# Latent queries of an encoder layer: rotary rows of four heads in one tile, the latent row factor as the exponent's scale

## The chip, the core and the metric

The kernel runs on one core of a Trainium2 chip. A core has a matrix engine (PE, with its weight loads listed apart as PEld), a vector engine (DVE), a scalar engine (ACT), a general engine (POOL), a queue engine that issues DMAs (SP), and 16 DMA engines. The engines run side by side and wait for one another by semaphores. The metric is the device time of one execution in microseconds, and less is better.

## The reference

The reference is one layer of a streaming encoder for 1024 prompt rows and 32 sample rows (1056 columns in the kernel, which keeps activations transposed). The branch that matters here is multi-head latent attention with 8 heads. Queries come from a latent of 384 numbers, keys and values from a latent of 256; a query and a key have 64 plain columns ("nope") and 32 columns that are turned by a rotary table; the turned key is shared by all heads.

```python
q = (rms_norm(q_lat, g_q_lat) @ w_uq).reshape(B, T, H_A, NOPE + ROPE)   # 384 -> 8 heads x (64 + 32)
q_nope = q[..., :NOPE]
q_rope = apply_rope(q[..., NOPE:], cos, sin)     # (x1*cos - x2*sin, x2*cos + x1*sin), halves of 16
...
s = (einsum(q_nope, k_nope) + einsum(q_rope, k_rope)) * MLA_SCALE       # 96 ** -0.5
p = softmax(where(mask, s, NEG))                  # block-causal, blocks of 64 rows
out = einsum(p, v)
```

The norm of the query latent divides each row by one number, its root mean square. That division is the "latent row factor": it is the same for all columns and all heads of a row, so it can be applied to the latent, to the queries, or to the scores.

## The kernel before

The work is in float32 precision by pairs: a matrix is split into a high and a low part, and a product is three matmuls (lines 75 to 77: high by high, low by high, high by low). `hi` (line 68) is an ACT copy, `lo` (line 71) a DVE subtraction.

The latent attention runs over four pairs of heads (`p` = 0 to 3). Before a pair's attention, its *expansion* has made queries, keys and (once for two pairs) values. Expansion 0 runs before the loop, as a stage of its own; expansion p + 1 is spread as fill work through the attention of pair p. An order is written out as a list of short names, and PE, ACT and DVE follow it for the work inside attention; elsewhere a scheduler orders the instructions of each engine by dependencies and its own estimates. Names in the list: S scores of a block, M its maximum, m the minimum of two pieces' negated maxima, E the exponent, R and C the reciprocal and the scaling, T transposes, h and v their high and low copies, V the product with values, o and p the output's copies and store; and as fill x and z (query matmuls of the pair's first and second head), X (queries times the table), J and j (high and low part of the finished queries, QH and QL), y, H, L (keys: matmuls, high, low), Z, I, i (sample rows and weight splits). U, W, w, f and G are fill from the output projection of the other branch. The digits after a name are the block of 128 query rows, and, after the point, the head of the pair.

Queries before: each head has a tile of 128 rows, 64 nope, 32 rotary, and the same 32 with halves swapped (the weight columns are gathered that way by `PARTS`, line 42). That takes 9 matmuls for each of three column blocks of 352, so 27 per head and 54 per pair. Line 1405 multiplies the tile, straight out of PSUM, by a table `qt` whose rows hold 96^-0.5, the cosines, and the signed sines. The row factor `qr` (one value per column, spread to 128 partitions by a DMA) is multiplied into that table at line 1480. The keys' tile has its 32 rotary rows twice, so the contraction over 128 rows sums both halves of the rotation. The scores then are QH and QL against KH and KL (lines 1510 to 1515), and the exponent (line 915) takes a bias, the negated maximum, and no scale.

PSUM has eight banks: three named s, two mm, two tr, one pv. SBUF tiles named big (three) and A (five) are shared by many steps.

## Time and profile before

| | us |
|---|---|
| median of three runs | 1690.74 (1689.0 to 1691.93) |
| the profiled execution, whole | 1689.64 |
| its span in the profile | 1687.8 |
| expansion 0 (keys, values, queries of pair 0) | 569.5 to 587.2 |
| attention of pair 0, with expansion 1 | 587.2 to 645.4 |
| attention of pair 1, with expansion 2 | 645.4 to 705.5 |
| attention of pair 2, with expansion 3 | 705.5 to some 766 |

Times are counted from the start of the span. A row of the timeline gives start, duration, engine, line of the kernel, operation, and output<-inputs with shapes; the brackets behind it give the idle time ahead of it on that engine, with what ended it. Listed durations of matmuls overlap, since the array is pipelined, so the rate of a run of matmuls is read from their starts. Rows of DMAs give the size of one and the median time from issue to landing.

### The profile page before, as it was taken

The numbers are of one execution on the slowest core, as the hardware profiler recorded it, in microseconds if no ns is written. First come the engines' busy times: TensorE is split into PE (matmuls) and PEld (weight loads), VectorE is DVE, ScalarE is ACT, GpSimd is POOL, SyncE is SP. The second block draws the span as 40 slices with busy tenths as digits, with TensorE's granted clock in tenths as the row PEclk, the third lists the DMA queues.
The fourth block names the chain that finished last, engine by engine and source line by source line (L and its number), as shares of the span: only waits on it lengthen the run. The fifth ranks groups of instructions, "written<-read, shape, count | busy, mean of one in ns | idle before, by whom it ended". The sixth has DMA issues, their size and how long they took to land. (4 is left out here: it accounts for less than half of the span.)

```text
span 1687.8 us, 30267 instructions
## 1 busy us (share of the span) xinstructions
PE 1650.3 (98%) x11646; PEld 1514.1 (90%) x11646; DVE 1268.5 (75%) x2121; ACT 995.0 (59%) x1945; POOL 294.9 (17%) x569
## 2 busy tenths in 40 slices
PE   5999999999999999999999999999999999999997
PEld 3999999999998898998988799999999999877885
DVE  4865698989873777877766789877787777787456
ACT  4545687978874677776762575444444444545442
POOL 3113312111110311111000212212112112200013
PEclk8999999999999999999999999999999999999999
DMA  9335876576532521221374523433333333697643
GB/s 337 101 125 187 281 239 165 168 198 174 174 112 57 147 68 44 81 70 50 130 241 137 194 91 100 151 107 120 131 109 118 132 110 116 241 333 237 207 141 122
DMA packets 185729, 255.22 MB, mean 151 GB/s; under 512 B 14702, under 2 KB 125056, under 8 KB 185584
## 3 DMA queue, kind: packets, MB, share of 16 engines
q1 hardware_dynamic: 164944, 194.11, 36.8%
q0 software_dynamic: 20416, 59.08, 10.1%
q8 instruction: 92, 1.51, 0.4%
q14 instruction: 53, 0.43, 0.1%
q10 hardware_dynamic: 224, 0.09, 0.0%
HBM read 187.86 MB, written 64.57 MB: 150 GB/s over the span
## 5 line engine op out<-in xcount | busy, mean ns | idle before, releaser
L68 ACT ACTIVATE wh<-wr 128x1024 fp32r<-128x1024 f32 (+5 forms) x163 | 132.1, 819 | 226.2 <-PE s L2066 82.4
L71 DVE TENSOR_TENSOR wl<-wr,wh 128x1024 fp32r<-128x1024 f32 (+5 forms) x163 | 150.2, 929 | 80.6 <-ACT wh L68 80.5
L75 PE MATMUL mm<-hh,wh 128*128 128x352 f32 x456 | 152.3, 334 | 0.0
L76 PE MATMUL mm<-hl,wh 128*128 128x352 f32 x456 | 148.7, 326 | 0.4 <-DVE hl L333 0.3
L77 PE MATMUL mm<-hh,wl 128*128 128x352 f32 x456 | 148.3, 325 | 0.0
L2065 PE MATMUL mm<-T,wh 128*128 128x256 f32 (+1 forms) x376 | 108.1, 288 | 0.0
L2067 PE MATMUL mm<-T,wl 128*128 128x256 f32 (+1 forms) x376 | 107.1, 285 | 0.4 <-DVE wl L71 0.2
L2066 PE MATMUL mm<-T,wh 128*128 128x256 f32 (+1 forms) x376 | 106.6, 284 | 0.0
L2067 PE MATMUL s<-T,wl 128*128 128x256 f32 (+1 forms) x348 | 99.3, 285 | 0.0
L2065 PE MATMUL s<-T,wh 128*128 128x256 f32 (+1 forms) x348 | 99.2, 285 | 0.0
L2066 PE MATMUL s<-T,wh 128*128 128x256 f32 (+1 forms) x348 | 98.8, 284 | 0.0
L71 DVE TENSOR_TENSOR wl<-S,wh 128x1024 fp32r<-128x1024 f32 (+1 forms) x55 | 59.2, 1078 | 50.3 <-ACT wh L68 49.9
L76 PEld LDWEIGHTS mm<-hl,wh 128*128 128x128 f32 x456 | 86.4, 189 | 3.5 <-DVE hl L333 1.8
L75 PEld LDWEIGHTS mm<-hh,wh 128*128 128x128 f32 x456 | 86.3, 189 | 3.4 <-issue 2.1
L2206 DVE SCALAR_TENSOR_TENSOR u<-u,c,u 128x1058 f32<-128x1058 f32 x68 | 87.1, 1318 | 2.0 <-ACT u L2203 0.7
L77 PEld LDWEIGHTS mm<-hh,wl 128*128 128x128 f32 x456 | 86.3, 189 | 0.2
L806 PE MATMUL tr<-c,A 128*128 128x128 f32 x576 | 85.0, 272 | 0.3 <-DVE A L922 0.3
L68 ACT ACTIVATE wh<-S 128x1024 fp32r<-128x1024 f32 (+1 forms) x55 | 51.8, 944 | 48.4 <-PE s L2066 13.4
L2067 PE MATMUL tr<-T,wl 128*128 128x272 f32 (+1 forms) x272 | 77.7, 286 | 0.3 <-DVE wl L71 0.3
L2065 PE MATMUL tr<-T,wh 128*128 128x272 f32 (+1 forms) x272 | 77.8, 286 | 0.0
L2066 PE MATMUL tr<-T,wh 128*128 128x272 f32 (+1 forms) x272 | 77.3, 284 | 0.0
L2196 POOL COPY c<-u 128x2 f32<-128x2 f32 x44 | 26.6, 604 | 266.6 <-DVE u L2142 230.5
(760 smaller groups left out, 5831.5 us busy)
## 6 DMA issues: line engine op xcount, KB each, us to landing
wr<-in_w_up_dram SPq DMA_DIRECT2D x44, 512.0 KB, 4.2
dr<-in_w_down_dram SPq DMA_DIRECT2D x43, 512.0 KB, 5.4
wr<-in_w_in_dram SPq DMA_DIRECT2D x33, 512.0 KB, 6.7
A<-in_w_ada_dram SPq DMA_DIRECT2D x32, 512.0 KB, 6.2
wr<-gdn SPq DMA_DIRECT2D x30, 512.0 KB, 4.5
gdn<-u POOLq DMA_DIRECT2D x23, 512.0 KB, 5.2
gd<-nat POOLq DMA_DIRECT2D x48, 176.0 KB, 3.5
t<-gd SPq DMA_DIRECT2D x16, 528.0 KB, 6.0
```

The source lines that it names most:

```text
L68: self.nc.scalar.activation(out, in_, AF.Identity, scale=scale)
L71: return self.nc.vector.tensor_tensor(out, full, hi.bitcast(F32), ALU.subtract)
L75: m(ps, lh, rh, start=start, stop=False)
L76: m(ps, lh, rl, start=False, stop=False)
L77: self.pe = m(ps, ll, rh, start=False, stop=stop).ins
L806: self.nc.tensor.transpose(tr[:, (2 * s + q) * P : (2 * s + q + 1) * P], at[q][:, b * P : b * P + P], self.idt)
L2065: m(ps[:, :n], w[0][:, k], x[0][:, k, c], start=first and k == 0, stop=False, skip_group_check=True)
L2066: m(ps[:, :n], w[0][:, k], x[1][:, k, c], start=False, stop=False, skip_group_check=True)
L2067: i = m(ps[:, :n], w[1][:, k], x[0][:, k, c], start=False, stop=k == 3, skip_group_check=True)
L2196: nc.gpsimd.tensor_copy(self.CV[:, 0:2, cc], u[:, 1024:1026])
L2206: nc.vector.scalar_tensor_tensor(y, u[:, w : w + YW], self.cvT[:, w, cc : cc + 1], y, ALU.mult, ALU.add)
```

## The change

Queries: `queries()` now has the 64 nope columns of both heads in one 128-row tile, 27 matmuls per pair. `rotary()` has the 32 rotary columns of four heads in another, 27 matmuls, and is done in expansions 0 (heads 0 to 3) and 1 (heads 4 to 7) alone. `turned()` multiplies that tile by a cosine table and by a sine table (six DVE products of 128x352), and writes both results to DRAM (`rqc` and `rqs`, 528 KB each). `rows()` loads, for each head of a pair, its 32 rows of either into rows 64 to 128 of the head's query tile (four DMAs of 132 KB). The nope rows are copied from PSUM with the factor 96^-0.5, head 0 by DVE (X), head 1 by ACT (K).

Keys: the second copy of the rotary rows is now swapped in its halves of 16, so it meets the sine products of unswapped queries. This takes 15 copies on POOL's queue where 10 were, and 3 loads of the cached keys where 2 were.

Row factor: it is no longer multiplied into the table. It is loaded as columns (`qs`, one per block of 128 query rows, by five DMAs in place of one that spreads a row), and is the exponent's `scale`. The maximum must carry it as well: m becomes one operation with both, and a new DVE step n (128x1) stands behind M for the 32 blocks whose scores are in one piece.

Also: the table is loaded by 12 DMAs in place of one; the weights of an expansion by six (pairs 0 and 1) or three in place of two, and split by one operation each on ACT and DVE; the transposes of the cached latents (line 1607) stand ahead of pair 2 in place of pair 1. The order has a list of its own for pair 0 with the rotary matmuls (z) and products (B) of expansion 1 in its middle; the z of the tail are gone from all lists.

```diff
-PARTS = ((0, 0, 96), (96, 80, 16), (112, 64, 16))
+QS = 96 ** -0.5
...
+    ORDER_0 = """
...
+        f2 E4.1b f G f v3.0 z z z B B z z z B B z z z B B x s4.1 S5.1a M5.0b R4.1 m5.0 V3.0 C4.1
...
-        V5.0 T6.1 o5 T6.0 h6.1 R7.1 p5 y C7.1 h6.0 v6.1 z v6.0 H z H L V6.1 V6.0 L T7.0 o6 z h7.0 p6 z X z v7.0
-        z y X V7.0 y o7 p7 z H z H L z L X Z J j
+        y v5.0 J V5.2 M7.1 n7.1 V5.1 Z E7.1 j V5.0 T6.1 o5 T6.0 h6.1 R7.1 p5 y C7.1 h6.0 v6.1 v6.0 H H L V6.1
+        V6.0 L T7.0 o6 h7.0 p6 v7.0 y V7.0 y o7 p7 H H L L Z J j
...
             elif k == "m":
-                vec.tensor_tensor(mx[:, 0:1], mx[:, 0:1], mx[:, 1:2], ALU.min)
+                vec.scalar_tensor_tensor(mx[:, 0:1], mx[:, 0:1], mx[:, 1:2], self.qs[:, 2 * u + i : 2 * u + i + 1],
+                                         ALU.min, ALU.mult)
+            elif k == "n":
+                vec.tensor_tensor(mx[:, 0:1], mx[:, 0:1], self.qs[:, 2 * u + i : 2 * u + i + 1], ALU.mult)
             elif k == "E":
                 self.exp = nc.scalar.activation(A[:, c0 : c0 + m], banks[x][:, :m], AF.Exp, bias=mx[:, 0:1],
-                                                accum_out=sm[:, j : j + 1])
+                                                scale=self.qs[:, 2 * u + i : 2 * u + i + 1], accum_out=sm[:, j : j + 1])
...
-            def queries(e):
+            def queries():
                 for c0, n in self.BLK:
-                    q.append((e, c0, n, self.bank(next(banks))))
+                    ps = self.bank(next(banks))
+                    for e in range(2):
+                        q[e].append((c0, n, ps[64 * e : 64 * e + 64, :n]))
                     c = slice(c0, c0 + n)
                     for k in range(3):
-                        self.mm3(q[-1][3][:, :n], w[2][:, k, e], w[3][:, k, e], self.QLh[k][:, c], self.QLl[k][:, c], k == 0, k == 2)
+                        self.mm3(ps[:, :n], w[2][:, k], w[3][:, k], self.QLh[k][:, c], self.QLl[k][:, c], k == 0, k == 2)
                         yield
...
+            def rotary():
+                for c0, n in self.BLK:
+                    rb.append((c0, n, self.bank(next(banks))))
+                    c = slice(c0, c0 + n)
+                    for k in range(3):
+                        self.mm3(rb[-1][2][:, :n], w[6][:, k], w[7][:, k], self.QLh[k][:, c], self.QLl[k][:, c], k == 0, k == 2)
+                        yield
+
+            def turned():
+                x = [self.tl(M, [P, 5 * 256], F32, "VSm")[:, :T], self.tl(self.At, [P, BIG], F32, "big")]
+                for i in range(3):
+                    c0, n, ps = rb[i]
+                    for y, t, d in zip(x, (tc_, ts_), self.rqd):
+                        nc.vector.tensor_tensor(y[:, c0 : c0 + n], ps[:, :n], t[:, c0 : c0 + n], ALU.mult)
+                        if i == 2:
+                            nc.sync.dma_start(d[4 * p : 4 * p + 4].rearrange("h d t -> (h d) t"), y)
+                        yield
+
+            def rows():
+                for e in range(2):
                     qf[e] = self.tl(self.At, [P, BIG], F32, "big")
-                self.xt = nc.vector.tensor_tensor(qf[e][:, c0 : c0 + n], ps[:, :n], qt[:, c0 : c0 + n], ALU.mult).ins
+                    for r, d in zip((64, 96), self.rqd):
+                        nc.sync.dma_start(qf[e][r : r + 32], d[2 * p + e])
+
+            def q_copy(e):
+                if not qf:
+                    rows()
+                c0, n, ps = q[e].pop(0)
+                x = qf[e][0:64, c0 : c0 + n]
+                if e:
+                    nc.scalar.activation(x, ps, AF.Identity, scale=QS)
+                else:
+                    self.xt = nc.vector.tensor_scalar(x, ps, QS, None, ALU.mult).ins
...
         steps["I"]()
         steps["i"]()
+        for _ in range(3):
+            for k in "zzzBB":
+                steps[k]()
         for _ in range(2):
             for k in "yyHHLL":
                 steps[k]()
         Vs = values(0, raw, "mm s s")
-        with self.tc.issue_after(self.v_last[1]):
-            nc.vector.tensor_tensor(qt, qt, self.qr, ALU.mult)
         proj["O"]()
 
-        for k in "xxxXxxxXxxxXJjZ":
+        for k in "xxxXKxxxXKxxxXKJjZ":
             steps[k]()
```

Two places show how this moves instructions. The first is DVE at the end of expansion 0. Before, the table's product with the row factor (L1480) follows the last low part of the values (V), and the queries' products (L1405) follow it:

```order
748 L71 TENSOR_TENSOR V_7016<-s_7051,V_7016 128x4x64 [waits Activation_49]
749 L71 TENSOR_TENSOR V_7016<-mm_7068,V_7016 128x4x64 [waits Activation_49]
750 L1480 TENSOR_TENSOR qt<-qt,big_6928 128x1056 [waits DMAHW5_49,DMASW4_49]
751 L71 TENSOR_TENSOR wl_6968<-wr_7194,wh_6967 128x512
752 L1405 TENSOR_TENSOR big_7106<-s_7096,qt 128x352 [waits DVE_49,PE_49]
753 L1405 TENSOR_TENSOR big_7106<-mm_7108,qt 128x352 [waits PE_49]
754 L1405 TENSOR_TENSOR big_7106<-s_7119,qt 128x352 [waits PE_49]
```

In the changed kernel the rotary products (L1446, from banks mm_7010, s_7024 and s_7036; `VSm_7020` holds the cosine products, `big_7021` the sine products) stand in that place:

```order
741 L71 TENSOR_TENSOR V_7074<-s_7110,V_7074 128x4x64 [waits Activation_49]
742 L71 TENSOR_TENSOR wl_6990<-wr_7226,wh_6989 128x512 [waits Activation_49]
743 L71 TENSOR_TENSOR V_7075<-s_7110,V_7075 128x4x64 [waits Activation_49]
744 L1446 TENSOR_TENSOR VSm_7020<-mm_7010,tc 128x352 [waits DMAHW3_49,DMAHW5_49,DMAHW2_49,DMAHW0_49]
745 L1446 TENSOR_TENSOR VSm_7020<-s_7024,tc 128x352
746 L1446 TENSOR_TENSOR VSm_7020<-s_7036,tc 128x352
747 L1446 TENSOR_TENSOR big_7021<-mm_7010,KSm_6963 128x352 [waits DMAHW5_49,DMAHW6_49,DMAHW4_49,DMAHW7_49,DMAHW2_49,DMAHW1_49]
748 L1446 TENSOR_TENSOR big_7021<-s_7024,KSm_6963 128x352
749 L1446 TENSOR_TENSOR big_7021<-s_7036,KSm_6963 128x352
```

The matmuls that fill those three banks are now PE's first of the stage, ahead of the keys, and the products that empty them come after the last value copy. On SP the two writes to DRAM and the reloads follow them in this order, with the load of a weight in between:

```order
166 L1448 DMA rqc<-VSm_7020 128x1056
167 L1448 DMA rqs<-big_7021 128x1056
168 L83 DMA wr_7232<-in_w_proj_b_dram 128x4x128
169 L1455 DMA big_7164<-rqc 32x1056
170 L1455 DMA big_7164<-rqs 32x1056
171 L1455 DMA big_7167<-rqc 32x1056
172 L1455 DMA big_7167<-rqs 32x1056
```

The second place is PE at the end of pair 0's attention. Before, the last transposes (L806) and the last product with values (L820) had fifteen matmuls between them, twelve of them query matmuls (from the latent `lat`, of 352 columns):

```order
4017 L806 MATMUL tr_7920<-c_70,A_7839 128x128
4018 L75 MATMUL mm_7899<-lat_6212,wh_6965 128x352
4019 L76 MATMUL mm_7899<-lat_6215,wh_6965 128x352
4020 L77 MATMUL mm_7899<-lat_6212,wl_6966 128x352
...
4030 L75 MATMUL mm_7945<-lat_6216,wh_6965 128x512
4031 L76 MATMUL mm_7945<-lat_6218,wh_6965 128x512
4032 L77 MATMUL mm_7945<-lat_6216,wl_6966 128x512
4033 L820 MATMUL pv_7950<-ptd_6954,V_7015 128x256
4034 L820 MATMUL pv_7950<-ptd_6955,V_7015 128x256
```

Now three key matmuls stand there, and scores of the next pair (L1569 to L1574) that the scheduler has moved up:

```order
4039 L806 MATMUL tr_7999<-c_70,A_7923 128x128
4040 L75 MATMUL mm_8009<-lat_6216,wh_6987 128x512
4041 L76 MATMUL mm_8009<-lat_6218,wh_6987 128x512
4042 L77 MATMUL mm_8009<-lat_6216,wl_6988 128x512
4043 L1570 MATMUL s_8047<-KL_6984,QH_7940 128x256
...
4046 L1574 MATMUL s_8047<-KH_6983,QL_7956 128x256
4047 L1569 MATMUL s_8055<-KH_6983,QH_7940 128x256
4048 L820 MATMUL pv_8013<-ptd_6978,V_7074 128x256
4049 L1570 MATMUL s_8055<-KL_6984,QH_7940 128x256
```

The query matmuls are gone from the tail; the same happens at the ends of pairs 1 and 2.

162 lines of the change are left out of this document (93 added, 69 removed).

## The prediction

> **What bounds the kernel now.** I read the page's first part, then the busy time by stretch, then the timeline of single engines in the stretches the change touches.
>
> ```profile
> span 1687.8 us, 30267 instructions
> PE 1650.3 (98%) x11646; PEld 1514.1 (90%) x11646; DVE 1268.5 (75%) x2121; ACT 995.0 (59%) x1945; POOL 294.9 (17%) x569
> ...
> 569.50:587.20 17.70, 17.70 (x121) 17.12 (x118) 15.90 (x32) 10.20 (x21) 8.87 (x17) 1.00 0.56 133
> 587.20:645.40 58.20, 58.09 (x413) 52.88 (x411) 46.71 (x117) 43.32 (x106) 10.93 (x20) 1.00 0.21 58
> 645.40:705.50 60.10, 59.83 (x423) 54.12 (x420) 49.20 (x120) 44.75 (x111) 9.69 (x17) 1.00 0.23 67
> ```
>
> The last three rows are the first expansion (keys, values and queries of pair 0) and the attention of pairs 0 and 1: length, then busy time of PE, PEld, DVE, ACT and POOL, clock, DMA share. PE is busy all the time, at full clock. So two things count: how many matmuls are issued, and whether PE is ever made to wait. What one matmul is worth is read from starts, since listed durations overlap:
>
> ```profile
> 569.50 0.50 PE L75 MATMUL mm<-lat,wh 128*128 128x512 f32 x1
> ...
> 578.04 0.28 PE L77 MATMUL mm<-wh,lat 128*128 128x256 f32 x1
> 578.16 0.33 PE L75 MATMUL s<-lat,wh 128*128 128x352 f32 x1
> 578.32 0.33 PE L76 MATMUL s<-lat,wh 128*128 128x352 f32 x1
> ...
> 582.37 0.32 PE L77 MATMUL s<-lat,wl 128*128 128x352 f32 x1
> 582.53 0.49 PE L1335 MATMUL tr<-c,big 128*128 128x128 f32 x3
> 582.77 0.41 PE L75 MATMUL s<-lat,wh 128*128 128x352 f32 x1
> ...
> 587.23 0.28 PE L1510 MATMUL s<-KH,QH 128*128 128x256 f32 x1
> ...
> 587.51 0.36 PE L1515 MATMUL s<-KH,QL 128*128 128x256 f32 x1
> ```
>
> A 352-column matmul is listed at 0.33 but the next starts 0.16 later; 27 run from 578.16 to 582.53, 4.37 us. Keys and values fill 569.50 to 578.16, then come queries of head 0, three transposes (0.24), queries of head 1 (to 587.23), and the first score follows with no gap; its third matmul, the one with QL, is at 587.51.
>
> **The change, part by part.** *Matmuls.* A pair had 54 query matmuls. Now it has 27 for the nope columns, and pairs 0 and 1 have 27 more for rotary columns of four heads. Expansions 0 and 1 keep 54, expansions 2 and 3 lose 27 each: 54 x 0.162 = 8.7 us of issue. By the listed 0.33 it would be 17.8; the starts exclude that. But they are taken from the tails of pairs 1 and 2, and the tail of pair 0 gives its 27 to the middle of pair 0 (4.37 more there). What a tail gives back is limited by who it waits for next:
>
> ```profile
> 637.57 0.85 PE L820 MATMUL pv<-ptd,V 128*128 128x256 f32 x4
> ...
> 642.00 0.64 PE L820 MATMUL pv<-ptd,V 128*128 128x256 f32 x4
> ...
> 643.17 0.32 PE L75 MATMUL mm<-lat,wh 128*128 128x352 f32 x1
> ...
> 644.60 1.03 PE L1607 MATMUL tr<-c,VSm 128*128 128x128 f32 x8
> ...
> 637.18 0.56 DVE L71 TENSOR_TENSOR ptd<-tr,ptd 128x384 fp32r<-128x384 f32 x1
> 637.65 0.68 DVE L71 TENSOR_TENSOR PTl<-tr,PTh 128x512 fp32r<-128x512 f32 x1
> 638.25 1.38 DVE L71 TENSOR_TENSOR KL<-mm,KH 64x512 fp32r<-64x512 f32 x2
> 639.66 0.43 DVE L794 TENSOR_TENSOR o<-pv,o 64x256 f32<-64x256 f32 x1
> 640.12 0.53 DVE L1405 TENSOR_TENSOR big<-mm,qt 128x352 f32<-128x352 f32 x1
> 640.56 0.55 DVE L71 TENSOR_TENSOR ptd<-tr,ptd 128x384 fp32r<-128x384 f32 x1
> ```
>
> This is the end of pair 0. Without the query matmuls PE comes to V6 (637.57 now) a microsecond earlier, but ptd is ready at 637.74 and PTl at 638.33. V7.0 (642.00 now) needs the last ptd, which follows KL (to 639.63) and o (to 640.09) on DVE; the table product at 640.12 is gone, so ptd is done at 640.65. V7.0 and the last three key matmuls take 1.17 (642.00 to 643.17): the tail ends at 641.8 instead of 644.60, 2.8 us earlier. In the new order two score groups of the next pair stand inside it (over 0.3 each, by the starts from 587.23 to 587.51), which fill part of the wait. Bounds are 2.8 and 4.37; I take the middle, 3.6, for each of pairs 0, 1 and 2. So pair 0 is +4.37 - 3.6 = +0.8, pairs 1 and 2 are -3.6 each. The eight transposes at 644.60 move to the start of pair 2, and cost the same there.
>
> *The start of the MLA stage.* Rotary's 27 matmuls now come first, before keys, and their three PSUM banks are held until DVE has multiplied them by the tables. In DVE's new order these six products stand behind all products of keys and values. Then come two DMAs to DRAM, and four reloads that QH waits for. The rows that price it:
>
> ```profile
> 572.43 1.39 DVE L71 TENSOR_TENSOR KL<-mm,KH 64x512 fp32r<-64x512 f32 x2 [1.20 <-ACT KH L68]
> 573.85 1.39 DVE L71 TENSOR_TENSOR KL<-s,KH 64x512 fp32r<-64x512 f32 x2
> ...
> 580.07 0.41 DVE L71 TENSOR_TENSOR V<-mm,V 128x256 fp32r<-128x256 f32 x1
> 580.40 1.25 DVE L1480 TENSOR_TENSOR qt<-qt,big 128x1056 f32<-128x1056 f32 x1
> 581.57 0.69 DVE L71 TENSOR_TENSOR wl<-wr,wh 128x512 fp32r<-128x512 f32 x1
> 582.17 0.52 DVE L1405 TENSOR_TENSOR big<-s,qt 128x352 f32<-128x352 f32 x1
> 582.61 0.52 DVE L1405 TENSOR_TENSOR big<-mm,qt 128x352 f32<-128x352 f32 x1
> ...
> 585.39 1.23 DVE L71 TENSOR_TENSOR QL<-big,QH 128x1024 fp32r<-128x1024 f32 x1
> ...
> 582.68 1.06 ACT L68 ACTIVATE KH<-A 64x1024 fp32r<-64x1024 f32 x1 [2.87 <-DMA lat<-big]
> ...
> 584.30 1.06 ACT L68 ACTIVATE QH<-big 128x1024 fp32r<-128x1024 f32 x1
> ...
> x1d<-facc SPq DMA_DIRECT2D x8, 512.0 KB, 2.6
> ...
> pbd<-nat POOLq DMA_DIRECT2D x32, 132.0 KB, 2.1
> ...
> big<-ob SPq DMA_DIRECT2D x4, 264.0 KB, 2.8
> ...
> l2d<-q POOLq DMA_DIRECT2D x1, 528.0 KB, 3.1
> big<-l2d SPq DMA_DIRECT2D x1, 528.0 KB, 4.0
> ```
>
> Rotary runs 569.50 to 573.85, keys (2.8) to 576.65, the transposes to 576.95. KL's first product was done 1.4 us after the last key matmul, the second 2.8 after it; so the one free mm bank comes at 578.2 and the one free s bank at 579.6. Two banks must carry four value groups of 1.44 (12 starts 0.12 apart), each given back only after its two high and two low copies (about 0.4 each on ACT and on DVE): I get the four groups at 578.2, 579.64, 581.6 and 583.06. On ACT the rotary keys' KH (1.06) stands before the last high copies, on DVE wl (0.69) before the last low one, so that one ends at 587.75, against 580.48 now. The six table products start then; at 0.435 from start to start the cosine ones end at 589.15, the sine ones at 590.45. The last query group needs a bank freed by the fifth and is issued 590.05 to 591.5, so it is no longer what is late.
>
> What is late is the round trip: the sine write leaves at 590.45, and its reload can't start before it has landed. No row shows this transfer. Nearest for the write: 2.6 (same queue, 512 KB) to 3.1 (528 KB); for the reload of 132 KB: 2.1 (same size, the other direction) to 4.0 (528 KB from DRAM). I take 2.6 and, for its direction, the 2.8 of 264 KB: 5.4, between 4.7 and 7.1. The Trainium skill (DMA: Bandwidth & Descriptors, "Anatomy of one DMA") gives about 2.0 us fixed plus bytes at 436 GB/s, fitted for the GpSimd path: an estimate of 3.2 and 2.3, so 5.5 and a sum 0.1 higher; the rows, 2.6 to 3.1 and 2.1 to 4.0, lie on both sides of it. QH follows from 595.85 to 596.9, QL to 598.15. The third score matmul is then at 598.15 instead of 587.51: **+10.6 us**. Everything else of pair 0 is queued behind it on PE; on SP a weight load and the next pair's weights stand behind the two writes and the reloads, which nobody needs so soon; on DVE and ACT the splits of the other branch's output stand behind the products. Should DVE reach the products at 583 (no bank waits beyond those of before), it is +6; with the slowest transfer and the keys' KH some 2 us later (POOL now issues 12 and 3 copies for its rows in place of 8 and 2, and five small ones for the factor), +14.
>
> *The rest.* The factor goes from the queries into exp's scale. In one op of DVE (the combined minimum) it costs nothing beside the row; for the 32 score blocks of one piece a new product of 128x1 stands between maximum and exp.
>
> ```profile
> L913 DVE TENSOR_TENSOR mx<-mx 128x1 f32<-128x1 f32 x32 | 4.9, 152 | 0.2
> ```
>
> At 0.152 that is 4.9 us of DVE, which is idle 20% of these stretches. It reaches PE where exp is awaited, mainly in two blocks of each pair's start: 8 x 0.152 = +1.2, between 0 and 4.9. I cost at nothing: the copies by 96^-0.5 (in the place of the table products, half of them moved to ACT, which has 15 us to spare per pair); fewer weight splits; more weight and table DMAs on SP, which is covered as long as the loads of the next pair start a pair ahead (if not, some microseconds in one expansion); the pair-1 rotary's round trip, which has the tail of pair 0's attention in front of it.
>
> Sum: 10.6 + 0.8 - 7.2 + 1.2 = **+5.4**. The profiled run took 1689.64 (span and 1.84 around it), 1.1 below the median 1690.74, so 1695.0 by its own time and 1696.1 against the median.
>
> **Rivals.** *The round trip is hidden, and it gets faster.* If the products run soon after 576 (rotary done 573.85, tables loaded), values and queries are not held up and end at 587.2; then only three copies, QH and QL are exposed, since no second head's matmuls cover them: about +2.4 at the start. With tails giving all, 2.4 + 0 - 8.7 + 1.2 = -5.1: 1685.6. It decides where the products start before about 580. Matmul count speaks for it, the DVE order against it. The Trainium skill (same page, "Rules for kernel authors") says to issue a DMA early and wait late so that its fixed cost overlaps; by that rule the trip would cost nothing. No row can agree yet; the order speaks against it, since the products that feed the DMA are themselves late. *Both cancel:* bank waits shorter, +6 at the start and tails as forecast: 6 + 0.8 - 7.2 + 1.2 = +0.8, 1691.5, within 0.2% (3.4 us, about what can be told from no change). *A longer stall:* +14 at the start and 2.8 from each tail: 14 + 1.6 - 5.6 + 1.2 = +11.2, 1702. For it speaks the wait of 2.87 before KH at 582.68, which shows the rotary keys' copies already late.
>
> **How the numbers follow.** Forecast (+3.4 to +9) 0.50; longer stall 0.17; cancelled 0.16; hidden 0.17. Slower 0.67, same 0.16, faster 0.17. The likeliest alone spans 1694 to 1700; the range takes in the two rivals' points nearly whole, 1686 to 1702.5.
>
> **What would show it.** Right: the six products start at about 587.7; PE idle for several microseconds before the first score, released by QH or QL, and behind these by the reload of the sine rows; pairs 1 and 2 some 3 us shorter; V6 and V7.0 waiting for DVE. Wrong: products before 580; a tail that gains all 4.4 or nothing; waits on exp all through the pairs, which would make n a cost of several microseconds.

## The result: 1.6% slower, and the profile after

| | before | after |
|---|---|---|
| median of four runs each | 1691.34 us | 1718.08 us (1715.01 to 1720.49) |
| ratio, with its 95% interval | | 1.0159 (1.0137 to 1.018) |
| the profiled execution (its span) | 1689.64 (1687.8) | 1719.44 (1717.7) |

The kernel became 26.7 us slower where +5.4 was forecast. The direction was right; the time lies far outside the range.

The page's first part of the changed kernel:

```profile
span 1717.7 us, 30277 instructions
PE 1654.9 (96%) x11592; PEld 1508.9 (88%) x11592; DVE 1273.6 (74%) x2140; ACT 1007.2 (59%) x1945; POOL 297.9 (17%) x578
```

PE issues 54 matmuls fewer than before and is listed busy for 4.6 us more (at half clock in places, as seen below). Its busy time by stretch follows. The stretches are expansion 0; from there to the first score of the third block of pair 0 (S2.0a); from S2.0a of one pair to that of the next, twice; and on to the fifth score group of pair 3. Behind length come PE, PEld, DVE, ACT and POOL, then clock, DMA share and GB/s.

```profile
571.87:600.66 28.79, 19.02 (x122) 16.98 (x118) 16.41 (x36) 13.13 (x25) 15.99 (x31) 0.93 0.69 168
600.66:608.13 7.47, 7.08 (x31) 6.14 (x32) 5.84 (x14) 3.54 (x10) 0.32 (x1) 0.59 0.03 4
608.13:674.68 66.55, 59.41 (x404) 51.84 (x402) 49.08 (x120) 44.89 (x104) 8.42 (x16) 1.00 0.33 93
674.68:739.36 64.68, 62.01 (x435) 54.40 (x434) 53.30 (x134) 50.78 (x119) 8.72 (x16) 1.00 0.27 81
739.36:799.06 59.70, 55.22 (x380) 48.33 (x379) 47.27 (x122) 45.95 (x110) 9.29 (x17) 0.99 0.23 66
```

The same stretches of the kernel before:

```profile
569.50:587.23 17.73, 17.73 (x122) 17.15 (x118) 15.93 (x32) 10.20 (x21) 8.90 (x17) 1.00 0.56 133
587.23:591.69 4.46, 4.46 (x33) 3.75 (x32) 4.35 (x10) 3.82 (x9) 2.51 (x6) 1.00 0.35 67
591.69:650.24 58.55, 58.31 (x413) 53.05 (x412) 47.03 (x117) 43.63 (x107) 9.21 (x17) 1.00 0.19 54
650.24:714.74 64.50, 63.55 (x452) 57.93 (x451) 53.09 (x131) 47.40 (x118) 8.87 (x16) 1.00 0.24 70
714.74:771.77 57.03, 56.97 (x407) 52.41 (x406) 45.52 (x115) 42.68 (x107) 9.18 (x16) 1.00 0.25 74
```

The last two stretches issue fewer matmuls now (435 for 452, 380 for 407), and yet one is as long as before and the other longer. PE has stopped being the engine that is always busy. The stretch with the first pair is 8 us longer with 9 fewer matmuls: matmuls have moved into its middle, others have left its end, and PE stands idle for seven microseconds of it.

Who made PE wait, by the view of waits (total us, times, longest), from the start of the stage to the end of the attention; first before, then after:

```profile
PE s L1510 <- ACT A L915: 1.0, 2, 0.6
PE tr L806 <- DVE A L922: 0.3, 1, 0.3
PE pv L820 <- DVE o L794: 0.2, 1, 0.2
PE mm L76 <- DVE wl L71: 0.2, 1, 0.2
```

```profile
PE s L1569 <- ACT QH L68: 6.3, 1, 6.3
PE mm L75 <- DVE KL L71: 5.5, 3, 2.5
PE mm L75 <- DVE big L1446: 3.1, 3, 1.1
PE pv L820 <- DVE o L794: 2.1, 3, 0.9
PE tr L806 <- DVE PTl L71: 1.3, 3, 0.5
...
```

These five rows alone are over eighteen microseconds of waiting; before, there were less than 2 in all. The first was forecast, and so was the kind of the fourth (products with values that wait for DVE); the second and the third were not.

**Where the 26 us come from.** Each number of the next table is the start of a score group, counted from the first matmul of the MLA stage in the same run, less the same for the kernel before. Counting from the stage's start takes out what happened ahead of it: that start lay between 1.9 us earlier and 2.4 later than in the profile before. In e7, which is the kernel before up to there, it was 1.7 earlier; in the changed kernel's own profile it was 571.87 for 569.50, about half of it from one longer wait for an early weight transfer (1.33 us ahead of 221.30, 0.21 before). The first five columns are score groups of pair 0 (S0.0 the first of all, S7.1 the last of the pair), then come the third block and the last score of pairs 1 and 2, the fifth score group of pair 3 and the last score of all. From S7.1 to the S2.0a of the next pair is the end of a pair.

| run | S0.0 | S2.0a | S5.0a | S6.0 | S7.1 | p1 S2.0a | p1 S7.1 | p2 S2.0a | p2 S7.1 | p3 5th | last | median less median before |
|---|---|---|---|---|---|---|---|---|---|---|---|---|
| after | 11.1 | 14.1 | 14.5 | 22.9 | 23.9 | 22.1 | 24.3 | 22.2 | 24.4 | 24.9 | 26.2 | +26.7 |
| e1, products early | 4.7 | 7.8 | 8.2 | 16.7 | 17.6 | 15.8 | 18.1 | 16.0 | 18.1 | 18.6 | 20.4 | +22.3 |
| e2, filler 34 | 12.3 | 14.6 | 15.0 | 23.4 | 24.4 | 22.5 | 24.8 | 22.7 | 24.8 | 25.4 | 25.9 | +26.1 |
| e9, filler 47 | 12.0 | 11.8 | 13.1 | 21.6 | 22.6 | 20.8 | 23.1 | 22.2 | 24.4 | 24.4 | 24.1 | +23.1 |
| e3, rotary in tail | 10.7 | 14.1 | 14.6 | 14.7 | 15.7 | 17.2 | 19.8 | 17.7 | 19.8 | 19.9 | 19.6 | +23.9 |
| e4, factor alone | -0.1 | -0.3 | 1.3 | 1.7 | 1.7 | 1.8 | 4.3 | 5.6 | 7.4 | 8.0 | 9.3 | +11.0 |
| e6, scale operand alone | -0.1 | -0.3 | 0.4 | 0.8 | 0.8 | 0.7 | 1.8 | 2.1 | 3.4 | 3.4 | 3.5 | +5.3 |
| e5, without the factor | 10.9 | 14.3 | 13.6 | 21.6 | 22.3 | 20.2 | 21.3 | 18.7 | 19.1 | 19.2 | 19.9 | +21.5 |
| e7, tails alone | -0.1 | 0.3 | 0.3 | 0.3 | 0.3 | 0.3 | 0.3 | 2.1 | 2.3 | 1.9 | 2.1 | +0.5 |
| e8, other order | 10.5 | 14.1 | 13.6 | 13.3 | 14.2 | 14.6 | 15.2 | 13.4 | 13.3 | 12.9 | 12.5 | +13.5 |
| e10, trip hidden | 6.0 | 11.2 | 10.4 | 10.1 | 11.0 | 11.4 | 11.9 | 10.1 | 10.0 | 10.7 | 10.6 | +7.6 |

Read across, the changed kernel loses 11.1 before its first score and 3.0 right behind it; 8.4 in the middle of pair 0; about 7 little by little inside the four pairs; and the ends of the pairs give back 1.8, 2.1, and then take 0.6. That is 26.2, about the medians' 26.7.

**The start, row by row.** The timeline of DVE, SP, ACT and PE in the changed kernel:

```profile
590.33 0.52 DVE L1446 TENSOR_TENSOR VSm<-mm,tc 128x352 f32<-128x352 f32 x1
...
592.06 0.95 DVE L1446 TENSOR_TENSOR big<-s,KSm 128x352 f32<-128x352 f32 x2
...
593.03 0.32 SPq L1448 DMA_DIRECT2D rqs<-big  x1
...
596.96 0.32 SPq L1455 DMA_DIRECT2D big<-rqs  x1
...
599.55 1.06 ACT L68 ACTIVATE QH<-big 128x1024 fp32r<-128x1024 f32 x1 [2.29 <-DMA big<-rqs]
...
600.66 0.58 PE L1569 MATMUL s<-KH,QH 128*128 128x256 f32 x1 [6.30 <-ACT QH L68]
```

Its transfers of the sine rows (KB each, and the median us from issue to landing, over all that the kernel makes of them):

```profile
rqs<-big SPq DMA_DIRECT2D x2, 528.0 KB, 3.7
big<-rqs SPq DMA_DIRECT2D x8, 132.0 KB, 3.4
```

The products follow the last value copy at once (it runs from 590.00) and end at 593.0. The write takes 3.9 until its reload is issued, the reload 2.6 until QH starts: 6.55 from the last product's end (593.0) to QH, with the medians' 3.7 and 3.4 not far from it. From 594.4, when its last query matmul ends, PE has nothing to do. The 16 DMA engines were busy all the time from 593.17 to 596.58, at 324 GB/s, so the write shared them with other transfers; whether that is why it took 3.9 is not shown.

**Right behind the stall the clock is halved.** PE rows of the same 264-column matmuls, first inside the stretch from 600.66, then at its end:

```profile
604.38 0.42 PE L75 MATMUL mm<-ObH,wh 128*128 128x264 f32 x1
604.60 0.42 PE L76 MATMUL mm<-ObL,wh 128*128 128x264 f32 x1
...
606.94 0.28 PE L75 MATMUL mm<-ObH,wh 128*128 128x264 f32 x1
607.06 0.29 PE L76 MATMUL mm<-ObL,wh 128*128 128x264 f32 x1
```

They start 0.22 apart and then 0.12. The granted clock is 0.5 from 596.58 to 606.82, which is three times 3.41 us, and 1.0 after it. So the stall costs twice: once as idle time and again as slow matmuls. The Trainium skill (TensorE: Matmul & The Clock Gate, "What's actually happening") says that the clock is halved after an idle window of about 3.4 us, given back after a busy one, and that these windows run freely; the stretches of 3.41 agree. How much idle time it took here is told at the end.

**The middle of pair 0.** Rotary's matmuls of expansion 1, and the products that empty their bank:

```profile
637.74 0.32 PE L77 MATMUL mm<-lat,wl 128*128 128x352 f32 x1
639.11 0.43 PE L75 MATMUL mm<-lat,wh 128*128 128x352 f32 x1 [1.05 <-DVE big L1446]
...
638.10 0.53 DVE L1446 TENSOR_TENSOR VSm<-mm,tc 128x352 f32<-128x352 f32 x1 [1.74 <-PE mm L77]
638.54 0.52 DVE L1446 TENSOR_TENSOR big<-mm,KSm 128x352 f32<-128x352 f32 x1
```

The next nine matmuls wait until both products have read the bank of the last nine; the same wait follows ahead of 641.85 and 644.63. Nothing else stands between z's and B's in the list, and the other mm bank is held there by a projection that is half done (f; its next matmuls come only at 652.74).

### The profile page after: what moved, and what is told of

Read it like the earlier page. It is cut to its first block, busy times and chain, and to the rows that moved or that the text cites. A ratio compares the mean times of both kernels' runs of the same rounds, so it can differ in the third digit from the quotient of the medians.

```text
span 1717.7 us, 30277 instructions
## 1 busy us (share of the span) xinstructions
PE 1654.9 (96%) x11592; PEld 1508.9 (88%) x11592; DVE 1273.6 (74%) x2140; ACT 1007.2 (59%) x1945; POOL 297.9 (17%) x578
## 5 line engine op out<-in xcount | busy, mean ns | idle before, releaser
L68 ACT ACTIVATE wh<-wr 128x1024 fp32r<-128x1024 f32 (+3 forms) x151 | 130.2, 864 | 229.6 <-PE s L2129 84.1
L71 DVE TENSOR_TENSOR wl<-wr,wh 128x1024 fp32r<-128x1024 f32 (+3 forms) x151 | 148.4, 986 | 83.4 <-ACT wh L68 80.8
L806 PE MATMUL tr<-c,A 128*128 128x128 f32 x576 | 85.3, 273 | 2.1 <-DVE PTl L71 1.3
L68 ACT ACTIVATE wh<-S 128x1024 fp32r<-128x1024 f32 (+1 forms) x55 | 51.8, 943 | 48.7 <-PE s L2129 13.3
L934 ACT ACTIVATE A<-s,mx,lat 128x384 f32<-128x384 f32 (+5 forms) x96 | 64.1, 672 | 26.7 <-DVE mx L929 17.6
```

The lines of the kernel that those rows point to most:

```text
L68: self.nc.scalar.activation(out, in_, AF.Identity, scale=scale)
L71: return self.nc.vector.tensor_tensor(out, full, hi.bitcast(F32), ALU.subtract)
L806: self.nc.tensor.transpose(tr[:, (2 * s + q) * P : (2 * s + q + 1) * P], at[q][:, b * P : b * P + P], self.idt)
L934: self.exp = nc.scalar.activation(A[:, c0 : c0 + m], banks[x][:, :m], AF.Exp, bias=mx[:, 0:1], scale=self.qs[:, 2 * u + i : 2 * u + i + 1] ...
```

## The experiments

### The row factor as the exponent's scale

**e4: the kernel before, with the factor moved to the exponent and nothing else.**

```diff
-            nc.vector.tensor_tensor(qt, qt, self.qr, ALU.mult)
...
-                vec.tensor_tensor(mx[:, 0:1], mx[:, 0:1], mx[:, 1:2], ALU.min)
+                vec.scalar_tensor_tensor(mx[:, 0:1], mx[:, 0:1], mx[:, 1:2], self.qs[:, 2 * u + i : 2 * u + i + 1],
+                                         ALU.min, ALU.mult)
+            elif k == "n":
+                vec.tensor_tensor(mx[:, 0:1], mx[:, 0:1], self.qs[:, 2 * u + i : 2 * u + i + 1], ALU.mult)
             elif k == "E":
                 self.exp = nc.scalar.activation(A[:, c0 : c0 + m], banks[x][:, :m], AF.Exp, bias=mx[:, 0:1],
-                                                accum_out=sm[:, j : j + 1])
+                                                scale=self.qs[:, 2 * u + i : 2 * u + i + 1], accum_out=sm[:, j : j + 1])
```

> The kernel before with one part of the change alone: the latent row factor as the exponent's scale, in the combined minimum and in the 32 new 128x1 products; query tiles, tables' loads and orders as before. The prediction priced it at +1.2 (0 to 4.9). Theory: within 0 to +2 of the kernel before, 1691 to 1693, the product qt times factor (1.25 on DVE) gone. Rival (a product on every maximum that PE waits for, and slower exponents): +4 to +6.

Measured: 1699.82, ratio 1.0062 (1.0047 to 1.0077), +11.0 against the median before that was taken with it, 1688.83. The table shows how it comes: nothing up to the third block, then 1.7 by the end of pair 0, 4.3 by that of pair 1, 7.4 by that of pair 2, and 9.3. It isn't one wait but a little in every pair. What each instruction costs stands in the groups of the attention (busy us, mean ns of one, idle time ahead and what ended it), before:

```profile
L915 ACT ACTIVATE A<-s,mx 128x512 f32<-128x512 f32 x24 | 16.5, 689 | 2.2 <-DVE mx L911 1.6
L915 ACT ACTIVATE A<-s,mx 128x128 f32<-128x128 f32 x8 | 2.9, 368 | 0.1
...
L913 DVE TENSOR_TENSOR mx<-mx 128x1 f32<-128x1 f32 x32 | 4.9, 152 | 0.2
```

and with the factor (e4):

```profile
L919 ACT ACTIVATE A<-s,mx,lat 128x512 f32<-128x512 f32 x24 | 18.7, 780 | 3.8 <-DVE mx L917 3.4 <-DVE mx L914 0.4
L919 ACT ACTIVATE A<-s,mx,lat 128x128 f32<-128x128 f32 x8 | 3.7, 456 | 0.2
...
L914 DVE SCALAR_TENSOR_TENSOR mx<-mx,lat 128x1 f32<-128x1 f32 x32 | 6.8, 212 | 0.2
L917 DVE TENSOR_TENSOR mx<-mx,lat 128x1 f32<-128x1 f32 x32 | 5.1, 158 | 0.9
```

Each exponent takes 0.09 us longer, whatever its width (0.091 at 512 columns, 0.088 at 128): 96 of them, 8.7 us of ACT. The minimum takes 0.06 longer, and n adds 0.16 thirty-two times. The Trainium skill (ScalarE: Activation LUTs, "What ACT_TABLE_LOAD costs") states that each operand of one value per partition adds about 93 ns to an activation; the rows agree.

What follows: the factor by itself costs about 10 us (8 to 13 by the interval). The prediction's +1.2 fell, and so did the larger figure, +4 to +6, that I had put against it.

**e6: only the exponent's scale operand.** As e4, with the minimum as before and no n, so the maximum lacks the factor.

```diff
             elif k == "m":
                 vec.tensor_tensor(mx[:, 0:1], mx[:, 0:1], mx[:, 1:2], ALU.min)
+            elif k == "n":
+                pass
```

> The kernel before with the factor as the exponent's scale operand and nothing else: plain minimum, no 128x1 products (the maximum lacks the factor, so the exponents carry a wrong bias). It splits the 10.5 us of the factor. The exponent takes 0.09 more with the operand, 96 times (8.8 us of ACT); the products and the longer minimum are 32 x 0.158 and 32 x 0.06 (7 us of DVE). Theory (the exponent gates the score banks, so the operand is most of it): 5 to 7 us slower than the kernel before, ratio 1.003 to 1.004. Rival (the products between maximum and exponent are most of it): 1 to 3 us, ratio 1.001 to 1.002.

Measured: 1694.40, ratio 1.0031 (1.002 to 1.0041), +5.3. So the longer exponents are some 40 to 50% of the factor's cost (5.3 of 11.0 by the medians; by the table, which leaves out that this run's stage began 1.4 late, 3.5 of 9.3), and the rest is n and the longer minimum. All of these stand on the chain from a block's scores over its maximum to its exponent and the transposes that PE does next; the scores' banks are held that long.

**e5: the changed kernel without the factor.** The scale operand, n and the product in m are taken out of the changed kernel, so the factor is applied nowhere.

```diff
-                vec.scalar_tensor_tensor(mx[:, 0:1], mx[:, 0:1], mx[:, 1:2], self.qs[:, 2 * u + i : 2 * u + i + 1],
-                                         ALU.min, ALU.mult)
+                vec.tensor_tensor(mx[:, 0:1], mx[:, 0:1], mx[:, 1:2], ALU.min)
             elif k == "n":
-                vec.tensor_tensor(mx[:, 0:1], mx[:, 0:1], self.qs[:, 2 * u + i : 2 * u + i + 1], ALU.mult)
+                pass
...
-                                                scale=self.qs[:, 2 * u + i : 2 * u + i + 1], accum_out=sm[:, j : j + 1])
+                                                accum_out=sm[:, j : j + 1])
```

> The changed kernel with the latent row factor left out of the prompt's scores: plain minimum, no 128x1 products, no scale operand in the exponent (the factor is applied nowhere, so the softmax is that of unnormed queries). It times the rotary part of the change. The factor alone cost 10.5 us in the kernel before. Theory (the two parts add up): 26.7 - 10.5 = 16 us slower than the kernel before, ratio 1.0095. Rival (the factor's cost hides in the stalls of the changed kernel): 20 to 26 slower, ratio 1.013 or more.

Measured: 1710.55, ratio 1.0128 (1.0106 to 1.0151), +21.5. The rotary part alone is most of the loss. The two parts, +21.5 and +11.0, make more than the whole, +26.7: in the changed kernel the factor is worth only some 5 us by the medians, though the intervals of the two ratios overlap. By the table the time lost from p1 S2.0a to the last score, ends of pairs included, is -0.3 here and +4.1 in the changed kernel. That its other half lies under the stalls, which both would fill, fits this but is only argued.

### The start of the stage

**e1: the products early.** The six products follow the keys' low parts, and the values' low parts wait for them.

```diff
-        for _ in range(3):
-            for k in "zzzBB":
-                steps[k]()
+        for _ in range(9):
+            steps["z"]()
         for _ in range(2):
             for k in "yyHHLL":
                 steps[k]()
+        for _ in range(6):
+            steps["B"]()
```

> The changed kernel, but DVE runs the six rotary products of expansion 0 right behind the keys' low parts and ahead of the values' low parts. In the changed kernel they start at 590.3, the first score at 600.7 after PE stood idle 6.3 us, and PE runs at half clock until 606.8. Theory (the late products cause the stall, and the stall causes the half clock): products from about 582 to 584.6, reloads landed by about 591, first score near 594, PE idle under 3 us and no half clock there: 10 us faster than the changed kernel, 1708. Rival (the sine table, whose loads wait for the krope matmuls, or the round trip sets the time anyway): products not before 587, at most 3 us faster, 1715.

Measured: 1711.11, ratio 1.0123 (1.0103 to 1.0142), by the two ratios some 6 us better than the changed kernel. The products now run from here (DVE), while PE's first score still waits for QH:

```profile
580.81 0.53 DVE L1446 TENSOR_TENSOR VSm<-mm,tc 128x352 f32<-128x352 f32 x1
...
593.11 0.58 PE L1571 MATMUL s<-KH,QH 128*128 128x256 f32 x1 [2.86 <-ACT QH L68]
```

Counted from the stage's start the products come 8.3 us sooner and the first score 6.4. From the last product's end, 583.5, to QH, 592.0, it is 8.5 us now, more than the 6.55 before: ACT is busy without a break from 588.3 (KH of the rotary keys, a weight split and the nope copies stand ahead of QH), and the sine rows' two reloads are issued only at 588.56 and 588.98. They take 2.7 and 3.0 us to land, the second at about 592.0, just when ACT comes to QH: so both hold it, and one of them alone, made faster, would hardly have moved it. And the 3 us idle on PE came with half clock from 592.62 to 599.45, two stretches of 3.41. So the late products did cause most of the stall, as forecast, but some 5 us of it stay when they are early, and the half clock with them.

**e2 and e9: keep PE busy through the stall.** Matmuls that nobody reads, 34 (e2) or 47 (e9), behind the last query group.

```diff
+        ps = self.bank("pv")
+        for i in range(47):
+            with self.tc.issue_after(self.pe):
+                self.pe = nc.tensor.matmul(ps[:, :352], AB[0][0][:, 0:P], self.QLh[0][:, :352], start=True, stop=True).ins
```

> The changed kernel with 34 more matmuls of 352 columns, whose result nobody reads, issued on PE behind the last query matmul of expansion 0, in the 6.3 us in which PE waits for QH. Theory (the idle itself lowers the granted clock, and the half clock from 596.6 to 606.8 costs the scores behind it some 3 us): clock 1.00 through the stage, 3 us faster, 1715, though PE does 5.5 us more work. Rival (the clock falls for another reason, or the stretch behind the stall waits for DVE and ACT and not for PE): no faster, 1718.

e2: 1714.92, ratio 1.0158 (1.0137 to 1.0179). The filler ended too soon. It left gaps of 2.1 and 0.7 us, and a half-clock stretch came after all, only later (602.46 to 605.88). It doesn't decide between the two, so e9 repeats it with more filler.

> As e2_keep_warm, but with 47 idle matmuls in place of 34, so that PE works to about the moment when QH is there. With 34 the clock still fell, from 602.5 to 605.9, since PE had 2.1 and 0.7 us of waiting in the 3.4 us before. Theory (the clock is judged over stretches of 3.41 us, by how long PE worked in them): no half clock behind the first score, 2 to 3 us faster than the changed kernel, 1715 to 1716. Rival (the half clock costs nothing because DVE and ACT hold these scores up anyway): as the changed kernel, 1718.

e9: 1714.35, ratio 1.014 (1.0127 to 1.0154). The stretch from the first score to S2.0a, in e9:

```profile
597.37:601.60 4.23, 4.23 (x33) 3.67 (x32) 3.50 (x10) 4.00 (x9) 0.00 (x0) 1.00 0.00 0
```

4.23 us at full clock, as before the change (4.46), where the changed kernel took 7.47 at 0.59. So the half clock behind the stall costs 3 us, net of the filler 2.3, and keeping the array busy with useless work is enough to avoid it. Two half-clock stretches came later in this run, at the ends of pairs 0 and 1 (from 668.99 and 720.19), so the whole gains little: 3.6 us by the medians, and the intervals of the two ratios overlap.

**e8: keys, rotary, queries, then values; factor back in the tables.** Rotary's products of head 0 go straight into its query tile by a copy inside SBUF, without DRAM; expansion 1 has its rotary in the tail.

```diff
+        for x in (tc_, ts_):
+            nc.vector.tensor_tensor(x, x, self.qr, ALU.mult)
+        self.hi(qt, self.qr, scale=QS)
+        for _ in range(9):
+            steps["z"]()
+        for _ in range(6):
+            steps["B"]()
+        for k in "xxxXKxxxXKxxxXKJjZ":
+            steps[k]()
         Vs = values(0, raw, "mm s s")
```

> The shared rotary tile kept, with what the runs point at: the factor multiplied into the tables as before (so no scale operand and no products on the maximum); in expansion 0 keys, then rotary and query matmuls, and the values last, so that the trip of the rotary rows lies beside the values; rows of head 0 by one DMA inside SBUF; the rotary matmuls of expansion 1 in the tail of pair 0. Theory: start +1 to +2 against the kernel before, pair 0 +1, the ends of pairs 1 and 2 together -3 (they gave 2.1 and -0.6 with the factor in them): within 2 us of the kernel before, 1687 to 1691, no half clock in the stage. Rival (the stall at the start remains, since tables land at 579 and QH waits behind other work on ACT): 4 to 7 us slower, 1693 to 1696.

Measured: 1702.55, ratio 1.0079 (1.0062 to 1.0096). Half of the loss is gone (no factor, no waits in the middle), but the stage still starts 10.5 late, and at half clock in two places (586.03 to 592.86 and 599.69 to 606.51). DVE shows the first cause:

```profile
586.12 0.53 DVE L1447 TENSOR_TENSOR big<-s,KSm 128x352 f32<-128x352 f32 x1 [3.94 <-DMA lat<-big]
```

The sine products write a tile that POOL's queue still copies the keys' rotary rows from. PE waits 4.75 us for the bank that these products empty. Its second wait, 2.66 us right ahead of the first score, is for KH of the rotary keys, which stands behind the values on ACT. New waits, for a buffer and for a place in ACT's order, took the place of the old one.

**e10: e8 with the products in tiles that nobody holds,** the keys' rotary copy right behind QH, and the values written behind that copy.

```diff
-                x = [self.tl(self.At, [P, BIG], F32, "big") for _ in range(2)] if p == 0 else [tc_, ts_]
+                x = [self.tl(O, [P, T], F32R, g).bitcast(F32) for g in ("QH", "QL")] if p == 0 else [tc_, ts_]
...
-        with self.tc.issue_after(self.v_last[0]):
+        with self.tc.issue_after(self.qh):
             self.hi(KHs[0][64:128], self.KRp[64:128])
...
+        Vs = values(0, raw, "mm s s")
+        proj["O"]()
```

> As e8_hidden_start, but the products are written to the second buffers of QH and QL, which are free then, and not to a buffer that the keys' rotary rows are still being copied from (the sine products waited 3.9 us for that), and the keys' own rotary copy no longer stands behind the values on ACT. Theory (that wait is what is left of the stall): first score at about 590 in place of 599.5, no half clock, 11 to 13 us faster than e8: 1689 to 1692, within 3 us of the kernel before. Rival (the next wait takes its place, at the keys' copies, which land at 586, or at the value banks): first score at 594 or later, 1695 to 1699.

Measured: 1698.89, ratio 1.0053 (1.0039 to 1.0067). No wait of PE is for the trip any more. One of 2.34 us ahead of 581.27 is for the sine products, which empty its bank and follow their table on DVE; these come later:

```profile
592.02 0.38 PE L1576 MATMUL s<-KH,QH 128*128 128x256 f32 x1 [1.89 <-ACT KH L68]
593.45 0.39 PE L1577 MATMUL s<-KL,QH 128*128 128x256 f32 x1 [1.05 <-DVE KL L71]
595.60 0.66 PE L1576 MATMUL s<-KH,QH 128*128 128x384 f32 x1 [0.87 <-DVE V L71]
```

The first of these waits is for KH, which this edit itself puts behind QH on ACT. The first score comes 6.0 late, S2.0a 11.2 late, with half clock from 594.61 to 601.43 between them. So even with the round trip out of the way the start of the stage is 11 us behind, and nothing comes back afterwards: the rest of the row lies between 10 and 12. This is the best of the variants that keep the shared rotary tile, and it is slower than the kernel before.

### The middle and the ends of the pairs

**e3: rotary of expansion 1 in the tail of pair 0,** where the second head's matmuls were.

```diff
-        S5.0b G i h3.0 f2 E4.1b f G f v3.0 z z z B B z z z B B z z z B B x s4.1 S5.1a M5.0b R4.1 m5.0 V3.0 C4.1
+        S5.0b G i h3.0 f2 E4.1b f G f v3.0 x s4.1 S5.1a M5.0b R4.1 m5.0 V3.0 C4.1
...
-        C7.1 h6.0 v6.1 v6.0 H H L V6.1 V6.0 L T7.0 o6 h7.0 p6 v7.0 y V7.0 y o7 p7 H H L L Z J j
+        C7.1 h6.0 v6.1 z v6.0 H z H L V6.1 V6.0 L T7.0 o6 z B B h7.0 p6 z z v7.0
+        z y B B V7.0 y o7 p7 z H z H L z L B B Z J j
```

> The changed kernel, but in pair 0 the rotary matmuls and products of expansion 1 stand in the tail, where the second head's query matmuls stood before. In the changed kernel the stretch from the first score of block 5 to that of block 6 takes 17.5 us instead of 9.0: 4.4 of matmuls and three waits of 1.2 for the products, since one of the two mm banks is held. Theory: that stretch is back at about 9 and the tail of pair 0 takes about 2 us more than in the changed kernel (it gained only 1.8 by losing these matmuls): 6 us faster, 1712. Rival (the tail is bound by PE, so the matmuls cost their 4.4 there and the products wait again): 1 to 3 us faster, 1716.

Measured: 1712.72, ratio 1.0139 (1.0124 to 1.0154). Between S5.0a and S6.0 the loss is now 0.1 in place of 8.4; the tail loses 1.5 where it gave 1.8. The same 27 matmuls therefore cost 5 us less in the tail than in the middle: 8.4 is their own 4.4 and 4.0 more, of which the three waits for the products are 3.6 by the starts (639.11 comes 1.37 after the matmul ahead of it, where 0.16 is usual), while in the tail they take the place of waits. The theory's figures, 6 us and 1712, were right.

**e7: only the ends of pairs 1 and 2.** The kernel before, with only one query matmul left for each column block of the second head in expansions 2 and 3: 6 of 54 stay, and the 48 that are gone are 7.8 us by the starts.

```diff
-                        self.mm3(q[-1][3][:, :n], w[2][:, k, e], w[3][:, k, e], self.QLh[k][:, c], self.QLl[k][:, c], k == 0, k == 2)
+                        if e and p > 1:
+                            if k == 0:
+                                nc.tensor.matmul(q[-1][3][:, :n], w[2][:, k, e], self.QLh[k][:, c], start=True, stop=True)
+                        else:
+                            self.mm3(q[-1][3][:, :n], w[2][:, k, e], w[3][:, k, e], self.QLh[k][:, c], self.QLl[k][:, c], k == 0, k == 2)
```

> The kernel before with 48 of the 54 query matmuls of the second head left out of the ends of pairs 1 and 2 (each block keeps one of nine, so heads 5 and 7 have wrong queries); everything else as before. 48 x 0.161 = 7.7 us of issue. The prediction gave such a tail 3.6 of 4.37. Theory (PE then waits there for DVE and ACT, whose work at the end of a pair is not less): 2 to 4 us faster than the kernel before, 1685 to 1687. Rival (the tail is bound by PE): 6.3 to 7.7 faster, 1681 to 1683.

Measured: 1691.75 beside 1691.26, ratio 1.0005 (0.9996 to 1.0014). Taking the matmuls away gains nothing. Waits of PE there in e7, total, times, longest:

```profile
PE mm L75 <- DVE KL L71: 3.1, 2, 2.6
PE tr L75 <- ACT wh L68: 1.6, 1, 1.6
PE pv L820 <- DVE ptd L71: 1.1, 2, 0.5
...
```

The first score of pair 2 comes 6 us sooner than before, its third block 2 us later. In between the array waits for the copies of the next keys and of a weight (wh), and runs at half clock (702.68 to 709.51; an estimate of its cost is 3 us, since the array worked for 6.6 of these 6.83 us at half rate). So at the end of pair 1, where 1.8 us are lost, part of the missing gain went to the clock. At the end of pair 2 the clock stayed at 1.00, and there the gain is 0.4 of 3.9: the matmuls had mostly covered what DVE and ACT do there. The changed kernel's end of pair 1 shows the same chain:

```profile
670.33 1.18 ACT L68 ACTIVATE KH<-mm 64x512 fp32r<-64x512 f32 x2
671.41 1.04 ACT L68 ACTIVATE QH<-big 128x1024 fp32r<-128x1024 f32 x1
...
671.89 1.38 DVE L71 TENSOR_TENSOR KL<-mm,KH 64x512 fp32r<-64x512 f32 x2
...
673.41 0.36 PE L75 MATMUL mm<-ObH,wh 128*128 128x264 f32 x1 [1.93 <-DVE KL L71]
```

Theory and rival both expected too much here: some gain was in each one's figures, and there was none.

## Why the prediction was right in direction and wrong in size

| step of the prediction | forecast | measured | |
|---|---|---|---|
| start of the stage | +10.6 | +11.1 and 3.0 | mechanism right, size near; half clock missed |
| rotary in the middle of pair 0 | +4.4 | +8.4 | bank waits missed |
| ends of pairs 0, 1, 2 | -3.6 each | -1.8, -2.1, +0.6 | wrong |
| exponents, n and drift inside the pairs | +1.2 | some +7 | wrong |
| sum | +5.4 | +26.2 | |

- **The start of the stage.** The forecast was set at the third score matmul, which came 12.0 later than before, counted from the stage's start. Less the 2.37 by which that start was late, the chain came as worked out: the four value groups at 578.33, 579.83, 581.89 and 583.38 (forecast 578.2, 579.64, 581.6 and 583.06), products at 587.96 (forecast 587.75), their end at 590.64 (590.45), the last query group at 590.26 (590.05). QH came 1.3 later than forecast, 597.18, since the trip took 6.55 and not 5.4: the write 3.9, above the 2.6 that I took from the nearest row, the reload 2.6 for my 2.8. The sum lies between the ends given, 4.7 and 7.1, but both rows for the write, 2.6 and 3.1, lay below what came. They lay below the 3.2 that the prediction works out from the Trainium skill as well, and not on both sides of it as it says. What failed is a term that the sum did not have: what becomes of the array's clock when it stands still this long. In this stage PE was never idle before, but the start of the same trace showed it: PE was busy for 0.98 us from 22.23 to 25.64, and the granted clock was 0.5 for the 3.41 us after. The Trainium skill did say it (the page named above). e9 puts it at 3 us.
- **"The tail of pair 0 gives its 27 to the middle" and +4.37 for them.** I costed the moved matmuls by their issue and did not follow the bank that they write. The order shows no other work between them, so the matmuls behind each group of nine wait for two products of DVE: 3.6 of the 4.0 us. e3 takes it away.
- **-3.6 for each tail.** This step is the largest miss, 7.5 us over three pairs. The bound of 2.8 came from letting V7.0 follow ptd sooner; I took the wait for KL and o on DVE to be as long as before and did not see that the next pair's work would wait for the same two engines. e7 shows that 7.8 us of matmuls there are worth nothing, some 3 of them because of half clock. Both bounds, 2.8 and 4.37, were too far on the good side; the end that was missing was zero.
- **"It costs nothing beside the row", "The factor goes from the queries into exp's scale", +1.2 for n.** The exponent's own price was left out: 0.09 us, 96 times, on the chain. The page of the Trainium skill that e4 names has that price; the sum had no term for an operand. e6 puts it at +5.3, e4 the whole factor at +11. Of the 7 in the table some 2 are not the factor's: e5, which has none, loses 2.1 inside the pairs by the same count. The forecast's own sign for this, waits on exp all through the pairs, came true: in the changed kernel ACT sat idle ahead of its exponents 17.6 us for m and 7.7 for n, in the kernel before 8.3 and 1.8 for the corresponding steps.
- **What was costed at nothing.** The additional transfers and the round trip of pair 1 made no wait of PE that any view shows between 594 and 860; that was right. The keys' KH that a rival named made no wait of PE ahead of the first score in the changed kernel; it did in e8 and e10 (2.66 and 1.89 us), where the trip is earlier.
- **The rivals.** "The round trip is hidden, and it gets faster" was tried with e8 and e10: in e10 it is hidden, and then it isn't faster, since keys and values come late. "A longer stall", +14 at the start, has the start's size by luck: the wait was as forecast, and the rest is the clock. "Both cancel" fell with the products, which came at 587.96 and not at 583.

What stays open: how much of the factor's 10 us hides in the changed kernel under other stalls, and which of the several buffers and queues would have to be moved for the start to come without any stall.

## What to carry to other kernels

An engine that is busy all the time is not yet a bound: before counting removed matmuls as gain, find out at that place what the other engines have to finish in the same time, and let zero be one of the bounds (e7: 7.8 us removed, none gained). Cost a moved group of instructions with the buffers that it writes and those who empty them, and cost an added operand of a repeated instruction on the chain at its own price, times its count. When a step leaves the matrix engine idle for two microseconds or more, add the slow stretch that can follow.

## What the runs showed of the hardware

- An exponent with a scale of one value per partition takes 0.09 us more than one without, at 128 and at 512 columns alike (368 to 456 ns, 689 to 780 ns).
- The granted clock of the matrix engine went to one half in stretches of 3.41 us or a multiple of it. Within one run their starts lie whole multiples of 3.413 us apart: from 596.58 to 797.97 in the changed kernel it is 59 of them. So time falls into fixed windows, and what counts is how long the engine stands idle inside one, not how long a single pause is. Two windows of the changed kernel, at the ends of pairs 2 and 1 (behind the length come the busy time of PE and the columns as above):

```profile
794.55:797.97 3.42, 1.10 (x8) 1.10 (x9) 3.31 (x6) 2.84 (x8) 0.26 (x1) 1.00 0.26 77
671.67:675.09 3.42, 1.68 (x11) 1.29 (x11) 3.31 (x9) 2.84 (x9) 0.30 (x1) 1.00 0.42 99
```

  PE is idle for 2.3 us of the first, and half clock follows from 797.97 to 801.38. It is idle for 1.7 us of the second, and the clock stays at 1.00: the pause of 1.93 us ahead of 673.41 is cut in two by the window's border. Between 566 and 862 us the twelve profiles have 17 windows at full clock with 1.85 us of idle time or more, and half clock follows each; of all the other windows at full clock, with up to 1.84 us, only one was followed by it (1.25 us, in e9 ahead of 720.19).

  The idle window of about 3.4 us that the Trainium skill names (TensorE: Matmul & The Clock Gate, "What's actually happening") is longer than this idle time; here the measurement decides.

- A transfer of 528 KB to DRAM took 3.9 us until the queue could issue a reload of it, though transfers of 512 and 528 KB in the profile before had taken 2.6 and 3.1. One trip of two hops was 6.55 us.
